# Queries and keys of the first layer projected by feature, and rotated without transposes

## The chip, the core and the metric

One core of a Trainium2 chip runs the whole program. The metric is the device time of one execution in microseconds (us). The core has five engines with a queue of instructions each: TensorE (PE) multiplies matrices and transposes, VectorE (DVE) and ScalarE (ACT) work element by element, GpSimd (POOL) does small side work, SyncE (SP) issues transfers. Each engine takes its instructions strictly in the order in which the program was built; an instruction that waits for another engine holds up all that stands behind it in its own queue.

## The reference

A decoder trunk of two layers over 256 tokens with 1024 features, all in float32. Layer 0 attends with 16 heads of 64 features and a causal mask (with 256 tokens there is one block, so the block selection picks nothing else). Layer 1 attends in a sliding window of 128 with four shared key and value heads. Each attention is followed by a gated feed-forward part with a causal convolution. Partial rotary turns the first 16 features of every head:

```python
h = rmsnorm(x, attn_norm[l])
q, k, v = jnp.split(h @ w_qkv_a[l], 3, axis=-1)
q = partial_rope(heads(q, N_HEADS), cos, sin)   # first 16 of 64 features of a head:
k = partial_rope(heads(k, N_HEADS), cos, sin)   # r1 = x1*cos - x2*sin, r2 = x2*cos + x1*sin
o = moba_attention(to_bhsd(q), to_bhsd(k), to_bhsd(heads(v, N_HEADS)))
x = x + o @ w_o
x = x + conv_ffn(rmsnorm(x, ffn_norm[l]), ...)
```

## The kernel before

**Split products.** Every float32 operand of a large product is split into a high part and a low part (what the high part leaves over), and each product is made of three matmuls: high with high, high with low, low with high. Activations lie transposed, with features on the partitions (`hT`).

**Weight units.** The weights come in units of 128 x 2048 elements. For a unit, `prepare` puts pieces of two kinds into the queues: ACT copies a piece to its high part (`hi_part`, L157) and DVE subtracts to get the low part (`lo_part`, L160). The early units are cut into four quarters of 512 columns, later ones into two halves of 1024. Four units can be held at once. Units 2 and 3 hold the queries and keys of the first group of four heads, 4 and 5 those of the second group, 6 and 7 of the third, 8 and 9 half of the values, 10 and 11 the fourth group.

**Order.** The order of the instructions is written out by a clock of planned time: `chain` puts a list of steps with delays off, `tick` advances the clock by what PE is planned to do and issues the steps that have become due, and `require` issues a chain at once where its result is needed. At the start and in the first projections PE, ACT, DVE and SP keep exactly the order in which the Python code issues; `manual.close()` in `attention` ends that, and from there a scheduler may move instructions past each other.

**Layer 0.** After half of the values, `qk_group(0, ...)` projects the first group of queries and keys, with tokens as output rows (`proj`: the activations are the stationary operand, 512 weight columns move). The result goes through `rotate`: ACT copies it from PSUM and scales it by the token's reciprocal norm (`qk_out`, L869), DVE turns 16 of each 64 features (`rope`, L346 to L352, with the tables `cs` and `sn`), PE transposes four blocks of 128 x 128 (`to_feature`, L358), ACT takes the high part and DVE the low part of the transposes (L369, L364). `spread` copies the keys' parts of the first 128 tokens into a block-diagonal tile on POOL (`kd`, L847). `attention` then runs scores (L402 to L409), softmax on DVE and ACT, transposes of the probabilities (`probs_T`, L463) and the products with the values (`values`, L486); in between, `fill` takes projections of the next groups from `filler`, by the numbers of `rate`.

**Tables.** `tables` (L817 to L823) makes cosine and sine: DVE, POOL, one ACT sine (L819) and four small POOL operations.

**Norms.** `row_bcast` spreads the reciprocal norm of the tokens over all partitions with a product of `ones` and a diagonal tile (L715), ahead of each feed-forward part.

Of the kernel before, what the change touches and what calls it, by code (L numbers as in the profile page):

```python
# [14 lines left out]
P = 128  # L15
D = 1024
S = 256
# [43 lines left out]
def trunk(ctx: ExitStack, tc, x, xw, pos, cpk, fin, sinks, w, out):  # L61
# [309 lines left out]
    def rotate(o, n, b, hi, lo, key, copy, then=None, wait=750.0):  # L371
# [3 lines left out]
              (wait, lambda: rope(t.rearrange("p (h d) -> p h d", d=HD), 2 * n, b)),  # L375
              (1000.0, lambda: to_feature(t, n, b, hi, lo, key, then)))

    def attention(qk, ready, filler, lead, rate, msk, vcol, sink):


# [116 lines left out]
        fill(lead)  # L497
        manual.close()
        n_g = NH // 4
        state = scores(0)  # L500
        for g in range(n_g):
            pT = []
            for p in range(2):
                fill(rate(g)[p])
                pT.append(probs_T(2 * g + p, state[p]))
            fill(rate(g)[2])
            if g + 1 < n_g:
                state = scores(g + 1)
            values(g, pT)
        for _ in filler:  # L510
            pass
        return oT
# [195 lines left out]
    def row_bcast(rb, b):  # L708

        r = rstd_of(b)  # L710
        d = row3(P)

        def spread():
            t = bank("t")
            nc.tensor.matmul(t[:, :P], ones, d, start=True, stop=True)  # L715
# [3 lines left out]
        chain(("rb", b), (2000.0, lambda: nc.vector.tensor_scalar(out=d, in0=ident, scalar1=r, scalar2=None, op0=ALU.mult)),  # L719
              (300.0, spread))  # L720
# [56 lines left out]
    def first_parts(c):  # L777
        hi, lo = hx(hT, c)
        (src, raw), g = chunk(c), (g1 if c > 1 else g0)[:, c:c + 1]
        wh, wl = (t[:, (c % 4) * 512:(c % 4 + 1) * 512] for t in wq[c // 4])  # L780
        if c == 0:
            nc.vector.tensor_copy(wh, raw)
        nc.scalar.activation(hi, src, AF.Copy, scale=g)
        if c > 0:
# [51 lines left out]
            v_out(b, 0, v_acc[b])  # L836

    chain(("rs",), (3000.0, first_norm))
    chain(("tables",), (3010.0, tables))
    used(0)  # L840
    used(1)

# [21 lines left out]

    qk = {}

    def qk_out(t, b, o):
        require("rs")
        nc.scalar.activation(t, o, AF.Copy, scale=rs[b])  # L869

    def qk_group(g, u):
        hi, lo = quad(), quad()
        o = [bank("acc") for _ in range(NB)]

        def finish(b):
            rotate(o[b], 4, b, hi, lo, ("qk", g), lambda t: qk_out(t, b, o[b]),
                   None if b else lambda src, w: spread(g, src[:, 2:4], w), 750.0 if g else 450.0)

        gens = [proj(o[b], hT, b, cols512(u), (u, u + 1) if b else ()) for b in range(NB)]
        if g == 0:  # L880
            for pair in zip(*gens):
                yield sum(pair)
            finish(0)
            finish(1)
        else:
            for b in range(NB):
                yield from gens[b]
                finish(b)
        qk[g] = (hi[:, 0:2], lo[:, 0:2], hi[:, 2:4], lo[:, 2:4], lambda p: p, diagonal(g))

    def run(gen):
# [77 lines left out]
    def ready_b(oT):  # L969
        o_down.append(Down(U_OB, 4, oT, lambda i: require("o", i)))  # L970

    attention(qk, ready_b, filler_b(), 3500.0, lambda g: ((4200.0, 2200.0, 1400.0), (3200.0, 1800.0, 1200.0), (3200.0, 1800.0, 1200.0), (4000.0, 1800.0, 1500.0))[g], mask, lambda h: 2 * (h // 8) + h % 2, True)

    hT = new_hT()
    y = [quad(F32, "y") for _ in range(2)]
# [144 lines left out]
```

## Time and profile before

| | |
|---|---|
| median of 3 runs | 571.14 us (571.11 to 572.1) |
| the profiled execution | 570.39 us |
| its span, first to last instruction | 568.3 us |
| busy in the span | PE 98%, DVE 75%, ACT 67%, POOL 18% |
| mean granted TensorE clock | 0.999 |

The span is shorter than the execution's time by 2.1 us of start and end. A row of the timeline gives start and duration in us, engine, source line, operation, written and read tiles, shapes and count; what stands in brackets at its end is the idle time of the engine ahead of it and what ended that. Matmuls overlap in the pipeline, so the cost of one is the distance from its start to the next one's, not its duration. A window's row gives, for each engine, busy time and (x) instructions.

### The profile page before, as it was taken

How to read it: one execution, taken by the hardware profiler on the slowest of the kernel's cores; microseconds unless marked ns; L12 is line 12 of the kernel's file. 1: busy time of each engine (PE TensorE's matmuls, PEld its weight loads, DVE VectorE, ACT ScalarE, POOL GpSimd, SP SyncE). 2: the span in 40 equal slices, each digit the busy share in tenths (PEclk: the TensorE clock that was granted, in tenths of full speed). 3: DMA queues.
4: the chain of work that ended last, by engine and by line, in shares of the span. 5: the costliest groups of instructions: out<-in, count | busy, mean ns of one | idle time of the engine just before them, and what ended most of it. 6: DMA issues, size and time to landing. Idle time of an engine off the chain costs nothing.

```text
span 568.3 us, 10191 instructions
## 1 busy us (share of the span) xinstructions
PE 558.8 (98%) x3858; PEld 504.5 (89%) x3858; DVE 427.1 (75%) x927; ACT 380.0 (67%) x768; POOL 100.3 (18%) x124
## 2 busy tenths in 40 slices
PE   8999999999999999999999999999999999999995
PEld 7888888899999999988888988879999999988884
DVE  6798678599788888744469988788898888773414
ACT  6988777578577776743449798877667777663313
POOL 7321001011333321100002200001333332110003
PEclk9999999999999999999999999999999999999999
DMA  8974344442565565664542714242466655565201
GB/s 326 374 277 154 144 148 149 149 149 76 213 216 202 206 211 213 217 203 177 219 148 96 276 76 149 74 149 76 149 223 223 221 206 198 230 221 205 92 0 74
DMA packets 15311, 100.99 MB, mean 178 GB/s; under 512 B 1952, under 2 KB 2080, under 8 KB 3744
## 3 DMA queue, kind: packets, MB, share of 16 engines
q1 hardware_dynamic: 14976, 100.09, 48.4%
q8 instruction: 30, 0.49, 0.3%
q10 hardware_dynamic: 288, 0.26, 0.1%
q14 instruction: 17, 0.14, 0.1%
HBM read 99.30 MB, written 1.05 MB: 177 GB/s over the span
## 4 chain that ended last, share of the span: by engine, by line
PE 88%; DVE 5%; ACT 4%; issue 1%; POOL 1%; DMA 1%; DVEq 0%; POOLq 0%; ACTq 0%
PE acc L533 9%; PE acc L538 9%; PE acc L534 9%; PE u L628 6%; PE u L629 6%; PE u L627 6%; PE t L628 6%; PE t L629 6%; PE t L627 6%; PE acc L317 4%; PE acc L319 4%; PE acc L318 4%; PE acc L739 2%; PE acc L628 2%; PE acc L629 2%; PE acc L627 2%
## 5 line engine op out<-in xcount | busy, mean ns | idle before, releaser
L160 DVE TENSOR_TENSOR wl<-wr,wh 128x1024 fp32r<-128x1024 f32 (+1 forms) x208 | 221.0, 1080 | 68.1 <-ACT wh L157 67.7
L157 ACT ACTIVATE wh<-wr 128x1024 fp32r<-128x1024 f32 (+1 forms) x208 | 190.0, 946 | 75.0 <-PE acc L538 55.4
L533 PE MATMUL acc<-wh,q 128*128 128x512 f32 x238 | 94.5, 397 | 0.8 <-ACT q L492 0.7
L534 PE MATMUL acc<-wl,q 128*128 128x512 f32 x238 | 92.9, 390 | 0.0
L671 POOL TENSOR_TENSOR m<-m,m 128x256 f32<-128x256 f32 x44 | 60.2, 1367 | 182.2 <-DVE m L666 109.2
L628 PE MATMUL u<-q,wh 128*128 128x256 f32 x320 | 88.5, 277 | 0.0
L627 PE MATMUL u<-q,wh 128*128 128x256 f32 x320 | 88.2, 276 | 0.0
L629 PE MATMUL u<-q,wl 128*128 128x256 f32 x320 | 88.1, 275 | 0.0
L629 PE MATMUL t<-q,wl 128*128 128x256 f32 x288 | 79.2, 275 | 0.0
L627 PE MATMUL t<-q,wh 128*128 128x256 f32 x288 | 79.2, 275 | 0.0
L628 PE MATMUL t<-q,wh 128*128 128x256 f32 x288 | 79.2, 275 | 0.0
L538 PE MATMUL acc<-wh,q 128*128 128x512 f32 x238 | 76.9, 389 | 0.0
L628 PEld LDWEIGHTS u<-q,wh 128*128 128x128 f32 x320 | 60.1, 188 | 0.1
L627 PEld LDWEIGHTS u<-q,wh 128*128 128x128 f32 x320 | 60.0, 188 | 0.1
L629 PEld LDWEIGHTS u<-q,wl 128*128 128x128 f32 x320 | 60.1, 188 | 0.0
L317 PE MATMUL acc<-wh,q 128*128 128x512 f32 (+1 forms) x160 | 57.1, 357 | 0.0
L319 PE MATMUL acc<-wh,q 128*128 128x512 f32 (+1 forms) x160 | 55.4, 346 | 0.0
L318 PE MATMUL acc<-wl,q 128*128 128x512 f32 (+1 forms) x160 | 55.2, 345 | 0.0
L627 PEld LDWEIGHTS t<-q,wh 128*128 128x128 f32 x288 | 54.1, 188 | 0.0
L628 PEld LDWEIGHTS t<-q,wh 128*128 128x128 f32 x288 | 54.1, 188 | 0.0
L629 PEld LDWEIGHTS t<-q,wl 128*128 128x128 f32 x288 | 54.1, 188 | 0.0
L533 PEld LDWEIGHTS acc<-wh,q 128*128 128x128 f32 x238 | 44.7, 188 | 10.5 <-ACT q L492 1.6
(165 smaller groups left out, 995.1 us busy)
## 6 DMA issues: line engine op xcount, KB each, us to landing
wr<-in_w SPq DMA_DIRECT2D x90, 1024.0 KB, 4.8
first<-in_xw SPq DMA_DIRECT2D x5, 384.0 KB, 5.6
xr<-in_x SPq DMA_DIRECT2D x2, 512.0 KB, 8.3
first<-in_xw SPq DMA_DIRECT2D x1, 768.0 KB, 7.0
fin_t<-in_fin SPq DMA_DIRECT2D x1, 512.0 KB, 6.2
out<-ot SPq DMA_DIRECT2D x1, 512.0 KB, 2.6
first<-in_xw SPq DMA_DIRECT2D x1, 388.0 KB, 3.6
out<-m ACTq DMA_DIRECT2D x1, 256.0 KB, 2.1
```

Source lines behind the costliest of these rows:

```text
L157: nc.scalar.activation(wq[i][0][:, c], raws[i][:, c], AF.Copy)
L160: nc.vector.tensor_tensor(out=wq[i][1][:, c], in0=raws[i][:, c], in1=f(wq[i][0][:, c]), op=ALU.subtract)
L317: nc.tensor.matmul(o, xh[:, blk(b)], wh, start=(c == 0), stop=False)
L318: nc.tensor.matmul(o, xh[:, blk(b)], wl, start=False, stop=False)
L319: nc.tensor.matmul(o, xl[:, blk(b)], wh, start=False, stop=(c == KC - 1))
L533: nc.tensor.matmul(o, ph[:, blk(b)], hi[:, s_], start=first, stop=False)
L534: nc.tensor.matmul(o, ph[:, blk(b)], lo[:, s_], start=False, stop=False)
L538: nc.tensor.matmul(o, pl[:, blk(b)], hi[:, s_], start=False, stop=end)
L627: nc.tensor.matmul(o, hi[:, s_], xh, start=(c == 0), stop=False)
L628: nc.tensor.matmul(o, hi[:, s_], xl, start=False, stop=False)
L629: nc.tensor.matmul(o, lo[:, s_], xh, start=False, stop=(c == KC - 1))
L671: nc.gpsimd.tensor_tensor(out=h, in0=gs, in1=t[1], op=ALU.mult)
```

## The change

There are five parts.

1. In layer 0, `proj_f` takes the place of `proj` for queries and keys. Now 128 weight columns are the stationary operand and all 256 tokens move, so the result already lies by feature. A group has a bank for the keys (first) and one for the queries, of two times 256 columns each. `rotate_f` then turns on whole banks: a DVE shuffle of partitions swaps the halves of the rotated features (L419), three DVE operations multiply with the tables and add (L420 to L422), ACT takes the high part (L425), DVE the low part (L430). The ACT copy with the norm, the rope on 16 features and the transposes are gone.
2. The norm is now inside the tables. `new_tables` builds on POOL a tile with cosine and sine for every feature of two heads (ones and zeros where nothing turns: L383 to L387), ACT scales it by the norm (L393), PE transposes it in four blocks (L399), ACT copies it to SBUF (L404).
3. In both attentions, PE's order of scores, probabilities' transposes and values is fixed as written, with the second pair of transposes, the filler, the next scores and the values as one fixed stretch. The last group's `rate` in layer 1 goes from 4000, 1800, 1500 to 3600, 1200, 600.
4. In layer 0 both copies of the transposed probabilities are on ACT.
5. `row_bcast` issues its product 1500 instead of 300 planned ns behind the diagonal tile, and the second chunk of the first value weights is split between ACT and DVE.

```diff
+    def new_tables(rs_, key, *wait):
+        ex = mid().rearrange("p (b k e d) -> p b k e d", b=NB, k=2, e=2)
+        nc.gpsimd.memset(ex[:, :, 0, :, ROT:], 1.0)
+        nc.gpsimd.memset(ex[:, :, 1, :, ROT:], 0.0)
+        for k, t in enumerate((cs, sn)):
+            for e in range(2):
+                nc.gpsimd.tensor_copy(ex[:, :, k, e, :ROT], t)
...
+        def scale():
+            for b in range(NB):
+                nc.scalar.activation(sc[:, b], ex[:, b].rearrange("p k e d -> p k (e d)"), AF.Copy, scale=rs_[b])
+        def turn():
+            t = bank("t")
+            for b in range(NB):
+                for k in range(2):
+                    nc.tensor.transpose(t[:, k * S + b * P:k * S + (b + 1) * P], sc[:, b, k], ident)
+            tick(440)
+            chain(key, (300.0, lambda: copy(t)))
+        def copy(t):
+            nc.scalar.activation(new, t.rearrange("p (k t) -> p k t", k=2), AF.Copy)
+            tab[0] = new
+        chain(key, *wait, (0.0, scale), (1200.0, turn))
+    def rotate_f(o, hi, lo, key, tkey, then=None):
...
+        def turn():
+            require(*tkey)
+            c_, s_ = (tab[0][:, k].unsqueeze(1).to_broadcast([P, 2, S]) for k in range(2))
+            nc.vector.stream_shuffle(u, o, SWAP)
+            nc.vector.tensor_tensor(out=t3, in0=o3, in1=c_, op=ALU.mult)
+            nc.vector.tensor_tensor(out=u3, in0=u3, in1=s_, op=ALU.mult)
+            nc.vector.tensor_tensor(out=t, in0=t, in1=u, op=ALU.add)
+        def high():
+            nc.scalar.activation(hi, t3, AF.Copy)
...
+        def low():
+            nc.vector.tensor_tensor(out=lo, in0=t3, in1=f(hi), op=ALU.subtract)
...
+        chain(key, (150.0, turn), (2600.0, high), (700.0, low))
+    def proj_f(o, hT, wv, units=()):
+        for m in range(2):
+            om = o[:, m * S:(m + 1) * S]
+            for c in range(KC):
...
+                nc.tensor.matmul(om, wh, xh, start=(c == 0), stop=False)
+                nc.tensor.matmul(om, wh, xl, start=False, stop=False)
+                nc.tensor.matmul(om, wl, xh, start=False, stop=(c == KC - 1))
...
-                    if e:
+                    if e or not sink:
                         nc.scalar.activation(pT, tp[:, :3 * P], AF.Copy)
...
+            with tc.manual_schedule(engines={mybir.EngineType.PE}):
+                pT.append(probs_T(2 * g + 1, state[1]))
+                fill(rate(g)[2])
+                if g + 1 < n_g:
+                    state = scores(g + 1)
+                values(g, pT)
...
-              (300.0, spread))
+              (1500.0, spread))
...
+    def tables_a():
+        tables()
+        new_tables(rs, ("rt",))
+    chain(("rt",), (3010.0, tables_a))
...
+        gens = [proj_f(o[n], hT, cols128(u, 2, S - n * S), (u, u + 1) if n else ()) for n in range(2)]
         if g == 0:
+            for _ in range(KC):
+                yield sum(next(gen) for gen in gens)
+        for n in range(2):
+            yield from gens[n]
+            finish(n)
```

**Place 1: PE in the first group's projection.** Before, PE goes straight from the first group (banks acc_282 and acc_283) to the second (acc_381):

```order
L317 MATMUL acc_283<-wh_252,q_107 128x512
L318 MATMUL acc_283<-wl_253,q_107 128x512
L319 MATMUL acc_283<-wh_252,q_108 128x512
L317 MATMUL acc_381<-wh_329,q_105 128x512
L318 MATMUL acc_381<-wl_330,q_105 128x512
```

Now the table's transposes (L399, reading the scaled tile m_23_349) stand inside the first group, ahead of the last chunk of the first column half; 42 matmuls of this group stand ahead of them; behind them come three of the keys' bank acc_283, three of the queries' bank acc_284, then 24 and 24:

```order
L445 MATMUL acc_284<-q_107,wh_253 128x256
L446 MATMUL acc_284<-q_108,wh_253 128x256
L447 MATMUL acc_284<-q_107,wl_254 128x256
L399 MATMUL t_369<-ident,m_23_349 128x128 x4
L445 MATMUL acc_283<-q_107,wh_253 128x256
L446 MATMUL acc_283<-q_108,wh_253 128x256
L447 MATMUL acc_283<-q_107,wl_254 128x256
```

What PE had no part in before, the tables, now has four instructions in the middle of its queue.

**Place 2: ACT around the sine.** Before, the second group's first weight unit (wh_329) follows the sine (L819) at once:

```order
L743 ACTIVATE v_101<-acc_113,rstd_304 128x512
L743 ACTIVATE v_102<-acc_114,rstd_313 128x512
L819 ACTIVATE rb<-rb 128x32
L157 ACTIVATE wh_329<-wr_237 128x512 x4
L157 ACTIVATE wh_362<-wr_250 128x512 x2
```

Now the scaling of the table stands between them, and the copy of the transposed table (L404) behind the unit's second quarter (wh_359 is the same unit 4, wh_415 unit 5):

```order
L831 ACTIVATE v_102<-acc_114,rstd_329 128x512
L910 ACTIVATE rb<-rb 128x32
L393 ACTIVATE m_23_349<-m_22_342,rstd_320 128x256
L393 ACTIVATE m_23_349<-m_22_342,rstd_329 128x256
L157 ACTIVATE wh_359<-wr_238 128x512 x2
L404 ACTIVATE tab_350<-t_369 128x512
L157 ACTIVATE wh_359<-wr_238 128x512 x2
L157 ACTIVATE wh_415<-wr_251 128x512 x3
L425 ACTIVATE q_281<-m_26_410 128x512
```

ACT now takes the second group's first weights only behind the two scalings (L393), which read what POOL's four copies (L387) write.

**Place 3: DVE at the second group's weights.** Before, the rotation of the first group is eight small operations between the quarters of units 4 (wl_330) and 5 (wl_363):

```order
L160 TENSOR_TENSOR wl_330<-wr_237,wh_329 128x512 x4
L160 TENSOR_TENSOR wl_363<-wr_250,wh_362 128x512 x2
L346 TENSOR_TENSOR rb<-m_22_377,cs 128x128
L351 TENSOR_TENSOR rb<-m_22_377,sn 128x8x8 x2
L352 TENSOR_TENSOR m_22_377<-rb 128x8x16
```

Now the last quarter of unit 4 (wl_360) stands behind the rotation of the keys' bank, and the last two quarters of unit 5 (wl_416) behind that of the queries' bank:

```order
L160 TENSOR_TENSOR wl_360<-wr_238,wh_359 128x512 x3
L419 STREAM_SHUFFLE m_27_411<-acc_283 128x512
L420 TENSOR_TENSOR m_26_410<-acc_283,tab_350 128x512
L421 TENSOR_TENSOR m_27_411<-m_27_411,tab_350 128x512
L422 TENSOR_TENSOR m_26_410<-m_26_410,m_27_411 128x512
L160 TENSOR_TENSOR wl_360<-wr_238,wh_359 128x512
L160 TENSOR_TENSOR wl_416<-wr_251,wh_415 128x512 x2
L419 STREAM_SHUFFLE m_29_450<-acc_284 128x512
L420 TENSOR_TENSOR m_28_449<-acc_284,tab_350 128x512
L421 TENSOR_TENSOR m_29_450<-m_29_450,tab_350 128x512
L422 TENSOR_TENSOR m_28_449<-m_28_449,m_29_450 128x512
L160 TENSOR_TENSOR wl_416<-wr_251,wh_415 128x512 x2
```

Weight pieces that the second group needs have moved behind operations that wait for the first group's banks.

More of the change, by code (lines that the diff above doesn't have):

```diff
@@ L376, in rotate @@
               (1000.0, lambda: to_feature(t, n, b, hi, lo, key, then)))
+    tab = [None]
+    def new_tables(rs_, key, *wait):
[5 more added lines that the diff above has]
+                nc.gpsimd.tensor_copy(ex[:, :, k, e, :ROT], t)
+        sc = mid().rearrange("p (b k f) -> p b k f", b=NB, k=2)
+        new = quad(F32, "tab")[:, :2]
+        def scale():
[12 more added lines that the diff above has]
+        chain(key, *wait, (0.0, scale), (1200.0, turn))
@@ new lines, in trunk @@
+    SWAP = [(i + HALF) % ROT if i < ROT else i for i in range(32)]
+    def rotate_f(o, hi, lo, key, tkey, then=None):
+        t, u = mid(), mid()
+        t3, u3, o3 = (a.rearrange("p (c t) -> p c t", c=2) for a in (t, u, o))
+        def turn():
[7 more added lines that the diff above has]
+            nc.scalar.activation(hi, t3, AF.Copy)
+            if then is not None:
+                then(hi, 0)
+        def low():
+            nc.vector.tensor_tensor(out=lo, in0=t3, in1=f(hi), op=ALU.subtract)
+            if then is not None:
+                then(lo, 1)
+        chain(key, (150.0, turn), (2600.0, high), (700.0, low))
@@ new lines, in proj_f @@
+    def proj_f(o, hT, wv, units=()):
+        for m in range(2):
+            om = o[:, m * S:(m + 1) * S]
+            for c in range(KC):
+                for b in range(NB):
+                    require("x", b, c // 4)
+                xh, xl = hx(hT, c)
+                wh, wl = wv(c, m)
+                nc.tensor.matmul(om, wh, xh, start=(c == 0), stop=False)
+                nc.tensor.matmul(om, wh, xl, start=False, stop=False)
+                nc.tensor.matmul(om, wl, xh, start=False, stop=(c == KC - 1))
+                tick(3 * S / 2.4)
+                if m and units and (c + 1) * len(units) % KC == 0:
+                    used(units[(c + 1) * len(units) // KC - 1])
+                yield 3 * S / 2.4
@@ L378, in attention, with cols128, wv @@
+    def cols128(u, n_u, at):
+        def wv(c, m):
+            i, r = divmod(c * n_u, KC)
+            need(u + i)
+            w_ = UNIT * n_u // KC
+            s_ = slice(r // n_u * w_ + at + m * P, r // n_u * w_ + at + (m + 1) * P)
+            return tuple(t[:, s_] for t in wq[u + i])
+        return wv
     def attention(qk, ready, filler, lead, rate, msk, vcol, sink):
@@ L499, in attention @@
         n_g = NH // 4
-        state = scores(0)
+        with tc.manual_schedule(engines={mybir.EngineType.PE}):
+            state = scores(0)
         for g in range(n_g):
             pT = []
[L503 to L509, printed above, removed]
+            fill(rate(g)[0])
+            pT.append(probs_T(2 * g, state[0]))
+            fill(rate(g)[1])
+            with tc.manual_schedule(engines={mybir.EngineType.PE}):
+                pT.append(probs_T(2 * g + 1, state[1]))
[3 more added lines that the diff above has]
+                values(g, pT)
         for _ in filler:
@@ L783, in first_parts @@
         nc.scalar.activation(hi, src, AF.Copy, scale=g)
-        if c > 0:
+        if c == 1:
+            nc.scalar.activation(wh[:, :S], raw[:, :S], AF.Copy)
+            nc.vector.tensor_copy(wh[:, S:], raw[:, S:])
+        elif c > 1:
             nc.scalar.activation(wh, raw, AF.Copy)
@@ L838, in trunk @@
     chain(("rs",), (3000.0, first_norm))
-    chain(("tables",), (3010.0, tables))
+    def tables_a():
+        tables()
+        new_tables(rs, ("rt",))
+    chain(("rt",), (3010.0, tables_a))
     used(0)
@@ L865, in trunk, with finish @@
     qk = {}
-    def qk_out(t, b, o):
-        require("rs")
-        nc.scalar.activation(t, o, AF.Copy, scale=rs[b])
     def qk_group(g, u):
         hi, lo = quad(), quad()
[L873 to L879, printed above, removed]
-        if g == 0:
[L881 to L888, printed above, removed]
+        o = [bank("acc") for _ in range(2)]
+        def finish(n):
+            c = slice(2 - 2 * n, 4 - 2 * n)
+            rotate_f(o[n], hi[:, c], lo[:, c], ("qk", g), ("rt",), None if n else lambda src, w: spread(g, src, w))
+        gens = [proj_f(o[n], hT, cols128(u, 2, S - n * S), (u, u + 1) if n else ()) for n in range(2)]
+        if g == 0:
+            for _ in range(KC):
[3 more added lines that the diff above has]
+            finish(n)
         qk[g] = (hi[:, 0:2], lo[:, 0:2], hi[:, 2:4], lo[:, 2:4], lambda p: p, diagonal(g))
@@ L970, in ready_b @@
         o_down.append(Down(U_OB, 4, oT, lambda i: require("o", i)))
-    attention(qk, ready_b, filler_b(), 3500.0, lambda g: ((4200.0, 2200.0, 1400.0), (3200.0, 1800.0, 1200.0), (3200.0, 1800.0, 1200.0), (4000.0, 1800.0, 1500.0))[g], mask, lambda h: 2 * (h // 8) + h % 2, True)
+    attention(qk, ready_b, filler_b(), 3500.0, lambda g: ((4200.0, 2200.0, 1400.0), (3200.0, 1800.0, 1200.0), (3200.0, 1800.0, 1200.0), (3600.0, 1200.0, 600.0))[g], mask, lambda h: 2 * (h // 8) + h % 2, True)
     hT = new_hT()
```

## The prediction

> **What bounds the kernel now.** I read the page's busy times and its chain first, then windows, then PE's timeline.
>
> ```profile
> span 568.3 us, 10191 instructions
> PE 558.8 (98%) x3858; PEld 504.5 (89%) x3858; DVE 427.1 (75%) x927; ACT 380.0 (67%) x768; POOL 100.3 (18%) x124
> PE 88%; DVE 5%; ACT 4%; issue 1%; POOL 1%; DMA 1%; DVEq 0%; POOLq 0%; ACTq 0%
> ...
> 14.00:28.00 14.00, 14.00 (x64) 11.58 (x63) 10.41 (x23) 12.66 (x27) 4.51 (x11) 1.00 0.93 372
> 28.00:42.00 14.00, 14.00 (x79) 11.74 (x78) 13.19 (x37) 12.22 (x21) 4.05 (x8) 1.00 0.76 285
> 440.00:500.00 60.00, 60.00 (x532) 60.00 (x531) 50.39 (x83) 43.02 (x71) 14.73 (x12) 1.00 0.60 217
> ```
>
> The reader is to see two things. PE is never short of work for long, so work taken from it shortens the end, and a wait put into its queue lengthens it: there is no idle time later to absorb one. And from 28 to 42 us, where the first heads are rotated, DVE (the third busy time) is at 13.19 of 14 us. Work added there has no room.
>
> **PE's work.** The timeline gives what a projection and a group of transposes cost.
>
> ```profile
> 16.41 0.39 PE L317 MATMUL acc<-wh,q 128*128 128x512 f32 x1
> ...
> 26.84 0.39 PE L318 MATMUL acc<-wl,q 128*128 128x512 f32 x1
> 30.01 1.03 PE L358 MATMUL t<-ident,m 128*128 128x128 f32 x8
> ...
> 44.75 0.60 PE L358 MATMUL t<-ident,m 128*128 128x128 f32 x4
> 45.10 0.47 PE L317 MATMUL acc<-wh,q 128*128 128x512 f32 x1
> 45.42 0.39 PE L318 MATMUL acc<-wl,q 128*128 128x512 f32 x1
> ```
>
> A matmul with 512 moving columns costs (26.84 - 16.41) / 46 = 227 ns. One with 256, in the feed-forward part, costs 60 / 532 = 113 ns (window 440 to 500). Queries and keys have 192 of the first, and now 384 of the second: 43.5 against 43.3 us, so -0.2. Four transposes cost 45.42 - 44.75 - 0.23 = 0.44 us with the matmul that they delay. Eight such groups go and one (the tables) comes: -7 x 0.44 = **-3.1**.
>
> **The wait for the tables.** This is the first of two terms that decide. The rows of ACT and POOL around the sine:
>
> ```profile
> 22.33 0.69 ACT L743 ACTIVATE v<-acc,rstd 128x512 f32<-128x512 f32 x1 [0.47 <-POOL rstd L303]
> 22.92 0.22 ACT L819 ACTIVATE rb<-rb 128x32 f32<-128x32 f32 x1
> 23.04 2.18 ACT L157 ACTIVATE wh<-wr 128x512 fp32r<-128x512 f32 x4
> 45.25 0.89 ACT L448 ACTIVATE m<-m,hst 128x256 f32<-128x256 f32 x2
> ...
> 23.20 0.20 POOL L822 COPY cs<-rb 128x16 f32<-128x16 f32 x1 [0.61 <-ACT rb L819]
> 23.73 0.77 POOL L823 TENSOR_SCALAR sn<-rb 128x16 f32<-128x16 f32 x1
> 4.41 0.45 POOL L758 COPY g<-first 128x8 f32<-128x8 f32 x1 [0.99 <-DMA first<-in_xw]
> ```
>
> Nothing that leads to the sine is changed: it starts at 22.9 us, and sine and cosine lie ready at 24.5. Then come four POOL copies (0.2 to 0.45 us each by L822 and L758, so 24.7 to 26.3 with some overlap; I take 25.2), two ACT scalings of 256 columns (0.45 each by L448: 26.1), and the last transposes with a handover: PE can go on at 26.4. Without the wait it would come to the transposes at 16.41 + 42 x 0.113 = 21.15 and be through at 21.6. So PE stands still for **+4.8** (4.3 to 5.9 from the ends above). Before, the first PE instruction that needed the tables (L358) came at 30.0 us. Whatever the split second chunk saves at the head only makes this wait longer, so I cost it at nothing.
>
> **The wait for DVE.** DVE's prices:
>
> ```profile
> 14.81 4.99 DVE L160 TENSOR_TENSOR wl<-wr,wh 128x512 fp32r<-128x512 f32 x8 [0.30 <-ACT wh L157]
> 28.58 0.29 DVE L346 TENSOR_TENSOR rb<-m,cs 128x128 f32<-128x128 f32 x1
> 28.79 0.35 DVE L351 TENSOR_TENSOR rb<-m,sn 128x64 f32<-128x64 f32 x2
> 29.18 0.29 DVE L352 TENSOR_TENSOR m<-rb 128x128 f32<-128x128 f32 x1
> 29.39 1.28 DVE L160 TENSOR_TENSOR wl<-wr,wh 128x512 fp32r<-128x512 f32 x2
> 31.28 0.69 DVE L364 TENSOR_TENSOR q<-t,q 128x512 fp32r<-128x512 f32 x1 [0.60 <-ACT q L369]
> 31.89 1.35 DVE L160 TENSOR_TENSOR wl<-wr,wh 128x1024 fp32r<-128x1024 f32 x1
> ...
> L782 DVE CAST wh<-first 128x512 fp32r<-128x512 f32 x1 | 0.4, 427 | 3.3 <-DMA first<-in_xw 3.3
> ...
> 133.72 0.84 POOL L671 TENSOR_TENSOR m<-m,m 128x256 f32<-128x256 f32 x1 [10.45 <-ACT m L670]
> 133.87 1.23 DVE L643 TENSOR_TENSOR q<-y,q 128x512 fp32r<-128x512 f32 x1
> ```
>
> An operation on two times 512 columns takes 4.99 / 8 = 0.62 from SBUF and 31.89 - 31.28 = 0.61 with PSUM. The old rotation cost 29.39 - 28.58 + 0.61 = 1.4 us of DVE for each block of 512. The new one has five operations, 3.1 us if the shuffle, which no row shows, costs like the others. Its bounds: 0.35 by the plain copy L782 less the usual overlap, 1.23 by L643, which ran beside POOL. It reads PSUM like L364, so I take 0.62. Four of the five are one turn of 2.5 us.
>
> Let PE go on behind the tables' transposes at R. The keys' bank needs 30 more matmuls, R + 3.4, and 0.2 to DVE. The turn of the keys ends at R + 6.1, the last quarter of unit 4 at R + 6.7, two quarters of unit 5 at R + 8.0, the turn of the queries at R + 10.5, the third quarter at R + 11.1, the fourth at R + 11.7. PE ends the first group at R + 54 x 0.113 = R + 6.1 and uses one quarter every 0.34 us; the low part of the seventh chunk (unit 5, third quarter) is wanted at R + 6.1 + 6 x 0.34 + 0.23 = R + 8.35. It waits 2.75, and 0.25 more at the next chunk: **+3.0** (2.4 to 4.3 by the shuffle's bounds, counted twice). Nothing of this depends on R. If the tables' transposes stood later on PE, DVE would still begin the keys' turn only after the third quarter (about 29 us, since ACT holds unit 4 back behind the tables), and PE would wait some 6.5 us at that chunk instead of 4.8 + 3.0.
>
> Behind that, DVE arrives at the softmax of groups 0 and 1 about when PE wants the probabilities. One copy of probabilities per pair moves from DVE to ACT and helps it there; ACT has room for the eight moved copies, since it loses as many copies of 512 columns (L869). I add **+0.7** (0 to 2) for waits of this kind. SP issues the transfer of a unit behind the last low part of an earlier one, so transfers slip with DVE; three raw units lie in stock, and I cost that at nothing.
>
> **Savings elsewhere.** The stalls that the other edits touch:
>
> ```profile
> 123.74 0.46 PE L715 MATMUL t<-m,ones 128*128 128x128 f32 x2 [0.28 <-DVE m L719]
> 387.61 0.46 PE L715 MATMUL t<-m,ones 128*128 128x128 f32 x2 [0.27 <-DVE m L719]
> ...
> 336.51 0.44 PE L358 MATMUL t<-ident,m 128*128 128x128 f32 x2 [0.42 <-DVE m L352]
> 373.33 0.50 PE L533 MATMUL acc<-wh,q 128*128 128x512 f32 x1 [0.69 <-ACT q L492]
> ```
>
> The later `row_bcast` puts eight or nine more matmuls (1.0 us) ahead of each L715, which covers both waits: **-0.6** (0 if the later `rb` makes DVE's scaling late). In layer 1 the values of the last group come six matmuls of 512 (1.4 us) earlier, so ACT's copy has cover, but its probabilities are also wanted 1.4 us earlier; the transposes at 336 us move away from the scores. Of 0.42 + 0.69 I take **-0.6** (-1.1 to +0.7).
>
> **The sum:** -0.2 - 3.1 + 4.8 + 3.0 + 0.7 - 0.6 - 0.6 = +4.0. The profiled execution took 570.39, so 574.4 in its terms; the median of the runs, 571.14, lies 0.75 above it, so **575.1** for the median. The ends: -3.3 + 4.3 + 2.4 + 0 - 0.6 - 1.1 = +1.7 (572.8) and -3.3 + 5.9 + 4.3 + 2 + 0 + 0.7 = +9.6 (580.7), not all at once.
>
> **Rivals.**
>
> The clock falls during PE's wait.
>
> ```profile
> 1.11 3.48 PE L251 MATMUL u<-ones 128*128 128x128 f32 x16 [1.11 <-DVE warm L227]
> 123.74 0.46 PE L715 MATMUL t<-m,ones 128*128 128x128 f32 x2 [0.28 <-DVE m L719]
> 123.95 0.36 PE L629 MATMUL u<-q,wl 128*128 128x256 f32 x1
> ...
> 561.83 0.28 PE L595 MATMUL u<-wh,q 128*128 128x256 f32 x1
> ...
> 562.20:567.20 5.00, 0.00 (x0) 0.00 (x0) 1.97 (x6) 1.31 (x4) 0.55 (x1) 1.00 0.48 184
> 567.50:568.30 0.80, 0.00 (x0) 0.00 (x0) 0.00 (x0) 0.00 (x0) 0.00 (x0) 0.50 0.00 0
> ```
>
> The same pair of records takes 0.21 us at 123.74 and 0.43 at the start, for 3.5 us: the array starts at half speed. At the end the granted clock was still 1.00 five us after the last matmul, and lower after that. PE's wait is idle for about 4.4 us. If the clock fell, some 3.5 us at half speed would cost +1.7, and DVE's turn would come later by as much: 576.8. The trace speaks rather against it; 15%. [...]
>
> DVE stays short through groups 0 and 1. If its new operations take over 0.75 us on average (L643's 1.23 beside POOL, whose `kd` copies fall into the turns), the softmax of group 1 comes after PE's transposes want it. Ten operations (two blocks' rotations) at 0.3 more each are +3.0, 578.1; 12%.
>
> The waits are shorter: POOL's copies overlap, the shuffle is as cheap as L782, the savings come in full: about 571.9, no change; 10%.
>
> The change does what it says and neither wait comes: -3.3 - 1.2 gives 566.6, faster. It needs the tables on ACT before 21 us, while the sine starts at 22.9, and a DVE with 2 x 2.5 us free where it has 0.8; 6%.
>
> My forecast holds the other 57%. The range reaches from the short waits to the long DVE queue: 571.5 to 579.0. A measurement of this kernel tells 0.2% (1.1 us) from no change, so 570.0 to 572.3 is no change: faster 0.06, same 0.12, slower 0.82.
>
> **What would show it.** Right: a PE gap of 4 to 6 us ahead of L399, released by ACT L393, at 21 us; a second gap of 2 to 4 us at a matmul L447 near 34 us, released by DVE L160; DVE over 13 of 14 us from 28 to 56; L358 down from 52 to 20 records. Wrong: PE idle under 2 us before 45 us, or shuffles (L419) well under 0.5 us with the quarters of unit 5 early. If both gaps are there and the time is still under 571, a saving elsewhere was missed.

## The result

The changed kernel takes 577.78 us (median of four runs, 576.3 to 578.27), the kernel before 571.12 us beside it: a ratio of 1.0108, with a 95% interval from 1.0087 to 1.013. That is 6.7 us slower, inside the predicted range and 2.7 us above the predicted time. The profiled execution took 577.91 us.

The page of the changed kernel, its busy times and the granted clock in 40 slices:

```profile
span 576.2 us, 10530 instructions
PE 560.7 (97%) x4022; PEld 514.7 (89%) x4022; DVE 438.0 (76%) x928; ACT 379.5 (66%) x771; POOL 103.5 (18%) x130
PEclk9889999999999999999999999999999999999998
```

The second and third digits of the last row are 8: the clock, which was 1.00 there before, fell early in the program. Two answers of windows over the changed kernel, the first with the stretches that the prediction used, the second cut where the granted clock changes (after the window: PE, PEld, DVE, ACT and POOL busy with their instructions, then the clock):

```profile
14.00:28.00 14.00, 10.25 (x68) 9.47 (x67) 7.67 (x17) 11.44 (x26) 4.27 (x17) 0.85 0.91 367
28.00:42.00 14.00, 11.37 (x79) 10.79 (x79) 10.49 (x19) 6.80 (x11) 2.52 (x3) 0.87 0.26 83
...
23.73:30.55 6.82, 5.21 (x25) 5.10 (x26) 1.99 (x3) 5.03 (x10) 1.19 (x8) 0.50 0.42 171
...
40.79:44.21 3.42, 3.42 (x18) 3.42 (x17) 3.38 (x4) 1.80 (x2) 2.07 (x2) 0.50 0.80 278
44.21:70.00 25.79, 25.79 (x225) 24.39 (x225) 24.73 (x63) 19.23 (x40) 4.99 (x8) 1.00 0.47 168
```

PE was busy for 14.00 of 14 us in the first two windows before, and now for 10.25 and 11.37. Twice the clock is at half, for 6.82 and 3.42 us, and from 44 to 70 us PE is busy without a break, although DVE is at 24.73 of 25.79. The whole loss arises before 44 us. PE's timeline shows its two waits and what a matmul costs behind the first:

```profile
21.32 0.28 PE L447 MATMUL acc<-q,wl 128*128 128x256 f32 x1
25.34 1.12 PE L399 MATMUL t<-ident,m 128*128 128x128 f32 x4 [3.75 <-ACT m L393]
...
26.47 0.41 PE L446 MATMUL acc<-q,wh 128*128 128x256 f32 x1
26.68 0.41 PE L447 MATMUL acc<-q,wl 128*128 128x256 f32 x1
...
36.22 0.28 PE L446 MATMUL acc<-q,wh 128*128 128x256 f32 x1
36.59 0.39 PE L447 MATMUL acc<-q,wl 128*128 128x256 f32 x1
...
36.93 0.28 PE L446 MATMUL acc<-q,wh 128*128 128x256 f32 x1
39.74 0.39 PE L447 MATMUL acc<-q,wl 128*128 128x256 f32 x1 [2.54 <-DVE wl L160]
```

By starts, the wait for the tables is 25.34 - 21.32 - 0.11 = 3.9 us. The wait for DVE is 39.74 - 36.93 - 0.11 = 2.7 us, with 36.59 - 36.22 - 0.11 = 0.26 ahead of it and 0.14 at the next chunk: 3.1 us. Behind the first, a matmul starts 26.68 - 26.47 = 0.21 us after the one before it instead of 0.113; so it is again from 40.8 to 44.2 us. The first fall comes at 23.73 us, still within the wait; of the 6.82 us at half clock PE works for 5.21. What released the first, on ACT and POOL:

```profile
23.09 0.22 ACT L910 ACTIVATE rb<-rb 128x32 f32<-128x32 f32 x1
24.78 0.91 ACT L393 ACTIVATE m<-m,rstd 128x256 f32<-128x256 f32 x2 [1.48 <-POOL m L387]
```

```profile
23.90 0.25 POOL L914 TENSOR_SCALAR sn<-rb 128x16 f32<-128x16 f32 x1
24.39 0.36 POOL L387 COPY m<-sn 128x32 f32<-128x32 f32 x2
```

And DVE's rows ahead of the quarter for which PE waits the second time:

```profile
31.89 0.74 DVE L419 STREAM_SHUFFLE m<-acc 128x512 f32<-128x512 f32 x1
32.52 0.68 DVE L420 TENSOR_TENSOR m<-acc,tab 128x512 f32<-128x512 f32 x1
33.11 0.69 DVE L421 TENSOR_TENSOR m<-m,tab 128x512 f32<-128x512 f32 x1
33.84 0.69 DVE L422 TENSOR_TENSOR m<-m,m 128x512 f32<-128x512 f32 x1
34.44 2.09 DVE L160 TENSOR_TENSOR wl<-wr,wh 128x512 fp32r<-128x512 f32 x3
36.47 0.73 DVE L419 STREAM_SHUFFLE m<-acc 128x512 f32<-128x512 f32 x1
...
39.00 1.29 DVE L160 TENSOR_TENSOR wl<-wr,wh 128x512 fp32r<-128x512 f32 x2
```

The order is the one forecast: the keys' turn, the last quarter of unit 4 with two of unit 5, the queries' turn, then the third quarter at 39.00, behind which PE goes on at 39.74. A turn takes 34.44 - 31.89 = 2.55 us, and the shuffle costs 0.63 of it, like its neighbours.

### The profile page after: what moved, and what is told of

It is laid out like the page before. It is cut to its first block, busy times and chain, and to the rows that moved or that the text cites. A ratio compares the mean times of both kernels' runs of the same rounds, so it can differ in the third digit from the quotient of the medians.

```text
span 576.2 us, 10530 instructions
## 1 busy us (share of the span) xinstructions
PE 560.7 (97%) x4022; PEld 514.7 (89%) x4022; DVE 438.0 (76%) x928; ACT 379.5 (66%) x771; POOL 103.5 (18%) x130
## 3 DMA queue, kind: packets, MB, share of 16 engines
HBM read 99.30 MB, written 1.05 MB: 174 GB/s over the span
## 4 chain that ended last, share of the span: by engine, by line
PE 89%; ACT 3%; DVE 3%; DMA 2%; issue 1%; POOL 1%; SPq 0%; DVEq 0%; POOLq 0%; ACTq 0%
PE acc L621 9%; PE acc L622 9%; PE acc L626 9%; PE u L715 6%; PE u L717 6%; PE u L716 6%; PE t L717 6%; PE t L715 6%; PE t L716 6%; PE acc L447 2%; PE acc L445 2%; PE acc L446 2%; PE acc L715 2%; PE acc L717 2%; PE acc L716 2%; PE acc L317 2%
## 5 line engine op out<-in xcount | busy, mean ns | idle before, releaser
L759 POOL TENSOR_TENSOR m<-m,m 128x256 f32<-128x256 f32 x44 | 63.8, 1449 | 177.2 <-DVE m L754 111.6
L621 PEld LDWEIGHTS acc<-wh,q 128*128 128x128 f32 x238 | 44.7, 188 | 9.6 <-issue 0.9
L626 PEld LDWEIGHTS acc<-wh,q 128*128 128x128 f32 x238 | 44.7, 188 | 9.3
L622 PEld LDWEIGHTS acc<-wl,q 128*128 128x128 f32 x238 | 44.7, 188 | 8.5 <-issue 0.2
L763 ACT ACTIVATE q<-m 128x256 fp32r<-128x256 f32 x44 | 18.1, 415 | 38.7 <-POOL m L759 38.7
```

The costliest lines, as they stand in the source:

```text
L621: nc.tensor.matmul(o, ph[:, blk(b)], hi[:, s_], start=first, stop=False)
L622: nc.tensor.matmul(o, ph[:, blk(b)], lo[:, s_], start=False, stop=False)
L626: nc.tensor.matmul(o, pl[:, blk(b)], hi[:, s_], start=False, stop=end)
L759: nc.gpsimd.tensor_tensor(out=h, in0=gs, in1=t[1], op=ALU.mult)
L763: (3400.0, lambda: nc.scalar.activation(hi, h, AF.Copy)),
```

## The experiments

All edits are to the changed kernel unless another is named. The kernel before, run beside them on the same chips, took 570.7 to 570.9 us. The first four take the two waits and the clock apart.

**Work for PE in the first wait.**

```diff
         def turn():
+            warm_up(20)
             t = bank("t")
```

> The changed kernel with 20 small matmuls of a constant tile put on PE right ahead of the tables' transposes, so that the array works through some 2 us of the wait; their result is not used. Theory (the clock falls because PE idles, and a slow stretch from 26.1 to 30.55 us costs 2.1 to 2.4 us): the wait for the tables keeps its length, since the sine and the scaling are where they were, the granted clock stays at 1.00 until 36 us, the wait at the seventh chunk of the second group stays at about 3.0 us, and the time falls from 577.8 to about 575.3. Rival, the record of the clock has nothing to do with PE's idling: half clock at 24 us again and 577.8. Rival, what PE gains before the first turn is given back at the seventh chunk: full clock at 24 us, a wait of about 5 us at the chunk, 577.8.

574.84 us (573.9 to 575.49). The timeline of PE in this run:

```profile
20.95 4.62 PE L251 MATMUL u<-ones 128*128 128x128 f32 x40
25.41 0.66 PE L400 MATMUL t<-ident,m 128*128 128x128 f32 x4
...
37.40 0.39 PE L448 MATMUL acc<-q,wl 128*128 128x256 f32 x1 [2.53 <-DVE wl L160]
```

The small matmuls fill the whole wait (20 of them leave 40 records and 4.46 us, not the 2 us I had taken), the transposes start no earlier, and the wait for DVE is 2.7 us as before. The clock stayed at 1.00 behind the tables (from 26 to 31 us, where the changed kernel has 0.54), and the time fell by 2.9 us. So in this kernel the slow clock came from PE's standing still. The four runs differ in the other fall, as far as the mean granted clock tells: two of them have 0.997 (573.9 and 574.46 us) and two 0.994 (575.22 and 575.49). The latter two, with the first fall alone gone, lie 2.4 us under the changed kernel, which is the expected price. In the profiled one, with 0.997, the clock did not fall behind the wait for DVE either (1.00 from 36 to 46 us), with the same wait of 2.7 us.

**Work in both waits.** The second place, `warm_at`, is the seventh chunk of the keys of the second group.

```diff
                 nc.tensor.matmul(om, wh, xl, start=False, stop=False)
+                if (m, c) == warm_at:
+                    warm_up(20)
                 nc.tensor.matmul(om, wl, xh, start=False, stop=(c == KC - 1))
```

> The same small matmuls a second time, ahead of the low part of the seventh chunk of the second group, where PE waits for DVE. Theory: both waits as they were (3.9 and about 3.0 us), no half clock anywhere, and another 1.6 us less than with the first lot alone: about 573.7, which is 2.6 above the kernel before and is the two waits less the saved transposes. If the 20 matmuls are not enough to count as work, the second fall stays and the time is that of the run with the first lot.

575.67 us: a miss of 2.0 us, by my price. The second lot takes 39.45 - 35.07 = 4.4 us by PE's starts, where the wait holds 2.7, and so makes PE late by 1.7 us itself. By the mean clock (0.997 to 0.999 in all runs, where the changed kernel has 0.989 to 0.991) neither fall came. With lots cut to the waits, 17 and 11:

> The run with two lots of small matmuls, with the lots cut to what the waits hold: 20 took 4.46 us of full clock, so 17 (3.8 us) ahead of the tables' transposes and 11 (2.45 us) ahead of the seventh chunk. Theory (each wait keeps its length and only the slow stretches go): no half clock before the end in any run, scores of the first group at about 44.0 us as in the run with the first lot, and every run near the lowest of that one: 573.9 to 574.3. The changed kernel then carries 577.8 - 574.0 = 3.8 us of slow clock and 3 us of bare waits over the saved transposes. Rival, the slow clock costs less and the runs with the first lot alone were only scattered: a median of 574.8 again, with a spread of 1.5.

574.21 us, and all four runs between 573.94 and 574.52 with a clock of 0.997 or above. The timeline:

```profile
21.07 3.96 PE L251 MATMUL u<-ones 128*128 128x128 f32 x34
25.19 0.84 PE L400 MATMUL t<-ident,m 128*128 128x128 f32 x4 [0.17 <-ACT m L393]
34.65 2.62 PE L251 MATMUL u<-ones 128*128 128x128 f32 x22
37.34 0.38 PE L450 MATMUL acc<-q,wl 128*128 128x256 f32 x1
```

Both waits are about as long as in the changed kernel (25.19 - 21.07 = 4.1 and 37.34 - 34.65 = 2.7 us), only filled. What is left out against it is the slow clock alone: 577.78 - 574.21 = **3.6 us**. Held against the kernel before that ran beside each of them (571.12 and 570.69) it is 3.1. The traces say 3.7, by the stage from the first projection to the first scores, which takes 27.65 us with filled waits (the row stands with the old turns below) and 31.33 us in the changed kernel:

```profile
16.66:47.99 31.33, 24.95 (x176) 24.07 (x175) 20.94 (x39) 16.73 (x33) 6.83 (x18) 0.84 0.51 197
```

**Tables ready early.** The scaling and the transposes of the tables run ahead of the first group, on constants.

```diff
+    new_tables((1.0, 1.0), ("rt",))
     v_first(KC - 1)
...
-    chain(("rt",), (3010.0, tables_a))
+    chain(("tables",), (3010.0, tables))
```

> The tables hold ones and zeros without sine, cosine or norm, so the rotation and the scaling with the norm are left out of the result; every instruction of the turns stays. The tables' scaling and transposes run before the first group, so PE has nothing to wait for there; POOL's four small copies are gone. Theory (the wait for DVE does not depend on the wait for the tables): no gap ahead of the first group's last chunk, no half clock at 24 us, but the wait of about 3 us at the seventh chunk of the second group and the fall of the clock behind it stay; 577.8 - 3.9 - 0.3 - 2.3 = about 571.3. Rival, DVE is late only because the tables are late: the second wait goes as well, about 566.7.

573.72 us. It is 2.4 above the forecast of the theory, mostly since the moved transposes still waited for ACT's scaling, 19.48 - 17.53 - 0.11 = 1.84 us by starts, and a quarter ahead of the seventh chunk another 0.3. The two sides that were to be told apart are told apart, by PE's timeline and a window:

```profile
19.48 0.74 PE L396 MATMUL t<-ident,m 128*128 128x128 f32 x4 [1.68 <-ACT m L390]
35.39 0.39 PE L444 MATMUL acc<-q,wl 128*128 128x256 f32 x1 [2.53 <-DVE wl L160]
```

```profile
36.70:40.12 3.42, 3.42 (x19) 3.42 (x18) 3.11 (x3) 1.54 (x2) 1.98 (x2) 0.50 0.88 307
```

With the tables out of the way the wait for DVE is still 2.7 us, and the clock still falls behind it. DVE is not late because the tables are late.

**A light turn.** The shuffle, the second product and the sum are left out, and with them the rotation.

```diff
-            nc.vector.stream_shuffle(u, o, SWAP)
             nc.vector.tensor_tensor(out=t3, in0=o3, in1=c_, op=ALU.mult)
-            nc.vector.tensor_tensor(out=u3, in0=u3, in1=s_, op=ALU.mult)
-            nc.vector.tensor_tensor(out=t, in0=t, in1=u, op=ALU.add)
```

> The turn has one DVE operation instead of four (the product with the first table); shuffle, product with the second table and sum are left out, and with them the rotation itself. The tables are made and waited for as in the changed kernel. Theory: the wait for the tables and the half clock behind it stay, the wait at the seventh chunk (3.0 us) goes, since 2 x 1.9 us of DVE work ahead of that quarter are gone, and with it the second fall of the clock (1.6): about 573.2. Rival, the second fall is an after-effect of the first: half clock again at about 38 to 41 us, 574.8. Rival, the quarter waits for ACT and not for DVE: about 577.

572.14 us (ten runs, 571.6 to 574.54). PE's and DVE's timelines, and a window:

```profile
20.73 0.28 PE L444 MATMUL acc<-q,wl 128*128 128x256 f32 x1
25.02 1.12 PE L399 MATMUL t<-ident,m 128*128 128x128 f32 x4 [4.01 <-ACT m L393]
```

```profile
30.69 0.69 DVE L419 TENSOR_TENSOR m<-acc,tab 128x512 f32<-128x512 f32 x1 [2.56 <-PE acc L444]
...
33.41 0.69 DVE L419 TENSOR_TENSOR m<-acc,tab 128x512 f32<-128x512 f32 x1
```

```profile
24.93:28.34 3.41, 3.33 (x16) 3.21 (x17) 1.99 (x3) 3.41 (x8) 0.00 (x0) 0.50 0.63 256
```

The wait for the tables is there, and one slow stretch behind it; the wait for DVE and the second slow stretch are gone (from 28.43 to 37.18 us a matmul starts every 0.11 to 0.12 us, and the mean clock is 0.995 where the changed kernel has 0.989). So DVE's turns make the second wait, and the second fall is no after-effect of the first. In this profile the clock was at half for 3.41 us only, against 6.82 in the changed kernel, which fits a time 1.1 us under the forecast. It is the profile of the shortest of the ten runs; two of the others have a mean granted clock of 0.990, as low as in the changed kernel (572.72 and 573.17 us), and what happened there is not shown.

**Tables asked for later.**

```diff
-        chain(key, *wait, (0.0, scale), (1200.0, turn))
+        chain(key, *wait, (0.0, scale), (5200.0, turn))
```

> The changed kernel with the tables' transposes asked for 5200 instead of 1200 planned ns behind the scaling: on PE they now stand behind all of the keys' bank of the first group (75 matmuls ahead of them instead of 42), at about 25.2 us, when the scaled tables are ready. Theory (the wait is DVE's in the end, and the tables' wait only takes a part of it in advance): nearly no wait at the transposes and full clock until 30 us, but DVE begins the keys' turn only at about 28 us, so the seventh chunk of the second group is waited for until about 35.5 us, 5 to 6 us instead of 3, with one or two slow stretches behind it; 573.5 to 574.5. Rival, the wait for the tables and its slow clock are the whole excess and the wait at the seventh chunk stays at 3.0: 577.8 - 3.9 - 0.3 - 2.3 = about 571.3.

574.28 us (573.61 to 574.99). PE's timeline:

```profile
25.29 0.84 PE L399 MATMUL t<-ident,m 128*128 128x128 f32 x4 [0.35 <-ACT m L393]
31.31 0.38 PE L447 MATMUL acc<-q,wl 128*128 128x256 f32 x1 [1.51 <-DVE wl L160]
...
35.86 0.58 PE L447 MATMUL acc<-q,wl 128*128 128x256 f32 x1 [2.53 <-DVE wl L160]
```

The wait for the tables is gone (0.35), and PE now waits for DVE three times, 1.7, 0.3 and 2.7 us by the starts, ahead of three quarters. The clock was at half for 6.8 us (0.50 from 34.89 to 41.72), part of it in the last of these waits. The rival's 571.3 did not come: of the 3.9 - 0.5 = 3.4 us that PE saves at the tables by starts, DVE takes back 1.6 (4.7 us of waits where the changed kernel has 3.1).

The next runs measure the rest of the change, and look for a better version.

**The old turns with everything else of the change.**

```diff
-        gens = [proj_f(o[n], hT, cols128(u, 2, S - n * S), (u, u + 1) if n else ()) for n in range(2)]
+        gens = [proj(o[b], hT, b, cols512(u), (u, u + 1) if b else ()) for b in range(NB)]
...
-    chain(("rt",), (3010.0, tables_a))
+    chain(("tables",), (3010.0, tables))
```

> The changed kernel with projection, rotation and tables of the kernel before (parts 1 and 2 undone); the fixed order in both attentions, the copies of the probabilities on ACT, the later norm product and the split second chunk stay. Theory (all of the loss is in parts 1 and 2; of the rest only the later norm product shows, 0.45 a layer): no half clock before the end, 0.9 less than the kernel before, so about 569.9 where that takes 570.8. Rival, the fixed order in layer 1 costs what the norm product saves: 570.8. Rival, part of the loss is in the other parts: over 572.

**568.85 us**, a ratio of 0.9962 (0.9949 to 0.9975) to the kernel before: faster than both kernels, and by 1.1 us better than I expected. PE has no wait over 0.2 us in layer 0, and the clock is full there. All of the loss is in parts 1 and 2. Layer 0 up to its feed-forward part, by stage, here and in the run with filled waits; each answer's first window goes from the first projection to the first scores, its second from there to the feed-forward part:

```profile
16.48:37.46 20.98, 20.98 (x100) 17.47 (x99) 16.88 (x37) 18.11 (x33) 5.64 (x12) 1.00 0.82 307
37.46:116.28 78.82, 78.82 (x468) 64.67 (x467) 55.60 (x166) 62.93 (x153) 6.57 (x13) 1.00 0.44 160
```

```profile
16.30:43.95 27.65, 27.31 (x232) 26.36 (x231) 20.57 (x38) 16.72 (x33) 6.82 (x18) 1.00 0.60 229
43.95:121.30 77.35, 77.35 (x556) 67.36 (x554) 64.77 (x173) 61.24 (x148) 8.83 (x13) 1.00 0.46 168
```

At full clock the new turns cost 6.7 us up to the first scores and win 1.5 us behind them.

**The later norm product alone**, in the kernel before.

```diff
-              (300.0, spread))
+              (1500.0, spread))
```

> The kernel before with one number changed: the product that spreads the norm is issued 1500 instead of 300 planned ns behind its diagonal tile. Theory (the gain of the run with the old turns, 2.0 us, is mostly this): both waits of 0.44 us at that product go and the feed-forward parts behind them start without the small gaps at their head, 0.5 in layer 0 and 0.9 in layer 1 by the run with the old turns: 569.4 where the kernel before takes 570.9. Rival, the gain comes from the fixed order in the attentions and the copies on ACT: 570.4.

569.6 us, a ratio of 0.998 (0.9971 to 0.999): 1.1 us of the 2.0. By starts the two waits were 123.74 - 123.18 - 0.11 = 0.45 us and 387.61 - 387.06 - 0.11 = 0.44 us; the 0.28 and 0.27 in the brackets count only from the end of the matmul before. The product that waited 0.27 us on DVE at 387.61 now stands in the timeline without a wait:

```profile
387.89 0.38 PE L715 MATMUL t<-m,ones 128*128 128x128 f32 x2
```

The other 0.7 to 0.9 us is not settled, and the intervals of the two ratios touch (0.9975 and 0.9971). The stage from the first scores to the feed-forward part is 0.2 us shorter with the fixed order and the copies on ACT than in the kernel before (78.82 against 79.04); one profile of the norm-only run also shows a wait of 0.5 us at 30.5 us, in code that is the kernel before's to the letter, so single profiles do not decide half a microsecond here.

**The fixed order undone in layer 1**, with the old turns; `sink` marks layer 1, and the last group's amounts of filler are 4000, 1800, 1500 again.

```diff
+        def fixed():
+            return ExitStack() if sink else tc.manual_schedule(engines={mybir.EngineType.PE})
...
-        with tc.manual_schedule(engines={mybir.EngineType.PE}):
+        with fixed():
             state = scores(0)
```

> The run with the old turns, with the fixed order undone in layer 1's attention alone (the scheduler orders PE there, and the last group's amounts of filler are those of before). Theory (the fixed order gains nothing in layer 1: it takes away waits of 0.58, 0.40 and 0.86 us and brings 1.38, 0.30 and 0.36): the waits of before come back and the new ones go, 568.5 to 568.9. Rival, the fixed order in layer 1 does gain, 0.6 as predicted: 569.5.

569.07 us, ratio 0.997 (0.9957 to 0.9983): no difference from the old turns with the fixed order (0.9962) that can be told. The waits of before (0.58, 0.40 and 0.86 us) are back in place of 1.38, 0.30 and 0.36. In the changed kernel the largest of the new ones is this:

```profile
341.61 0.55 PE L548 MATMUL u<-ident,m 128*128 128x128 f32 x3 [1.15 <-ACT m L554]
```

**New turns for the later groups only.** One or two groups of heads are turned in the old way, the tables are built later, and the other groups are turned in the new way.

```diff
     def qk_group(g, u):
+        if g < 2:
+            yield from qk_old(g, u)
+            return
...
-    chain(("rt",), (3010.0, tables_a))
+    chain(("tables",), (3010.0, tables))
+    chain(("rt0",), (16000.0, lambda: new_tables(rs, ("rt",))))
```

> The changed kernel with the old projection and rotation for the first two groups of heads and the new one for groups three and four; the tables are built later, where nothing waits for them. Theory: neither wait and no half clock, four groups of four transposes fewer and one more (-1.3), 0.9 for the norm products: about 568.6, 2.2 less than the kernel before. Rival, DVE is also short from 56 to 70 us (13.99 of 14 busy in the changed kernel), so the turns of the third group make PE wait there: 570 to 571.

> The same with the old way for the first group alone, so that three groups of heads are turned in the new way. Theory: the second group's turns come at about 40 us, when the early quarters of the weights are done, and make nobody wait; six groups of transposes fewer and one more (-2.2), 0.9 for the norm products: about 567.7. Rival, DVE (13.19 of 14 us busy from 28 to 42 before) has no room for one more turn there: a wait of 1 to 3 us ahead of the second group's scores, 569 to 571.

> Two groups turned in the old way and two in the new one, again with layer 1 left to the scheduler. Theory: as the run with two old groups, less at most 0.3: 568.4 to 568.9, since the transposes saved there (PE's end 0.95 us earlier than with all old turns) should show at last. Rival, what is saved in layer 0 is lost again at the end of the program: 569.0.

With two old groups: 568.95 us, ratio 0.9964 (0.9952 to 0.9976), and with layer 1 left to the scheduler as well 569.08 us. With one old group: 569.45 us, with a wait of 1.25 us ahead of the second group's scores as the rival has it, at a transposition of the first group's probabilities (L548) that is released by DVE. So two late groups in the new way cause no wait, but they do not beat the old turns in time, although PE's last matmul starts 0.95 us earlier than there (559.55 against 560.50). The end of the program took that back: the spans of the two profiled executions are 566.8 and 566.9 us. The last transfer, of 256 KB, landed 2.8 us after its issue with two old groups and 2.2 us with all old turns; in the run with two old groups and layer 1 left to the scheduler it was 2.5. Why is open; the code there is the same.

## Why the prediction was right, and where not

The direction, both waits, their places in PE's queue and their releasers came as forecast; the second began at 37 us instead of 34, behind the first slow stretch. Term by term, with the run that measures it:

| term | forecast, us | measured, us | from |
|---|---|---|---|
| wait for the tables | +4.8 | +3.9 | timeline of the changed kernel |
| wait for DVE | +3.0 | +3.1 | the same; 2.7 with early tables, gone with light turns |
| transposes and projection | -3.3 | about -2.0 | 27.65 + 77.35 (filled waits) - 20.98 - 78.82 (old turns) = 5.2, less waits of 4.1 + 3.1 there |
| softmax lateness | +0.7 | 0 | PE busy for 25.79 of 25.79 us from 44 us on, and no stall over 0.2 us before layer 1 |
| later norm product | -0.6 | -1.1 | norm alone |
| layer 1's attention | -0.6 | 0 | fixed order undone in layer 1 |
| slow clock | a rival, +1.7 | +3.6 | filled waits |
| rest of the change | 0 | -0.7 to -0.9 | old turns, less the norm; cause open |

The measured column adds up to +3.9 + 3.1 - 2.0 - 1.1 + 3.6 - 0.8 = +6.7. Several of its terms are differences between the same runs, so that it closes is no check of its own.

**The step that failed** is the first rival: "If the clock fell, some 3.5 us at half speed would cost +1.7", at 15%, with the remark that the trace speaks rather against it. The clock fell during the wait for the tables, for 6.8 us where the rival's estimate has 3.5, and it fell a second time, for 3.4 us, behind the wait for DVE, which I had not thought of as a candidate at all, since it is shorter. Two errors lie in it. I read from the end of the old trace that five idle microseconds leave the clock at 1.00, and took the wait as safe; and I left it out of the sum as another course of events, where it is a cost on top of the two waits. Without the slow clock the changed kernel takes 574.2 us, 0.9 under the predicted 575.1. That this lies so near is in part luck: the terms that came out lower than forecast (the wait for the tables, the softmax, the norm product, the rest of the change) do so by 2.9 us in all, and the others (the wait for DVE, the transposes, layer 1) came out 2.0 us higher.

**Sizes that were off.** The wait for the tables was put 0.9 too high: the fourth POOL operation ran for 0.25 us, not 0.77, so the copies began at 24.09 us instead of 24.5, and PE came to the transposes a little later, at 21.43 us instead of 21.15. The four copies took 0.7 us together, as assumed. The transposes were put 1.3 too high. Behind the first scores five groups go, by my price 2.2 us, and the stage became 1.5 us shorter. In layer 1 the moved values did lose their waits, but the second pair of transposes now waits 1.3 us for ACT's copy: an exchange, as the run without it shows. The later norm product was put at the idle times in the brackets, 0.28 and 0.27, where its two waits are 0.45 and 0.44 us by starts; the 0.2 that is left to 1.1 is within the noise.

One sign that I had named did not show: DVE over 13 of 14 us from 28 us on. It was busy for 10.49 of the first 14 and 12.91 of the next, since at half clock PE was late with the keys' bank, and DVE stood waiting for it (3.44 us ahead of 31.89).

**Steps that held to the tenth.** The shuffle's price (0.62 taken, 0.63 measured), the turn of 2.5 us, the place and the length of the wait for DVE, and that nothing of it depends on R: 2.7 us in the changed kernel, with early tables and with PE kept busy. That later transposes of the tables would only move the wait to DVE was said as "some 6.5 us at that chunk"; it came as 4.7 us over three quarters. DVE, nearly full from 44 to 70 us (24.73 of 25.79), made nobody wait there: that rival did not come.

## What to carry to other kernels

When a wait is put into the queue of an engine that was always busy, price the time after it as well: where the clock fell, the matmuls behind waits of 2.7 to 4.2 us ran at half clock for 3.3 to 5.9 us, and that was about half of this loss (3.1 to 3.7 of 6.7). A wait that is taken away is not gained in full where the engine that is late next has no room: with the tables asked for later, PE waited 4.7 us for DVE instead of 3.1. Look at what that engine has queued ahead of the wanted piece. And where an edit has several parts, run the side parts alone: here they were worth 2.0 us, and were hidden under a loss of 8.9.

## What was not expected of the hardware

The four changes of the clock in the first 70 us of the changed kernel, at 23.73, 30.55, 40.79 and 44.21 us, lie 6.82, 10.24 and 3.42 us apart: 2, 3 and 1 times 3.41. So I counted PE's work in windows of that length, laid out from a change that the trace shows: in the changed kernel, in the run with early tables (a change at 36.70 us), in the run with late tables (34.89), and in the kernel before at its end (567.34):

```profile
20.31:23.73 3.42, 1.29 (x12) 1.09 (x10) 0.66 (x5) 2.52 (x7) 2.10 (x7) 1.00 1.02 386
23.73:27.14 3.41, 1.80 (x9) 1.69 (x10) 0.90 (x2) 2.36 (x6) 1.19 (x8) 0.50 0.81 333
37.38:40.79 3.41, 1.05 (x6) 0.86 (x7) 3.38 (x6) 1.67 (x3) 0.00 (x0) 1.00 0.55 228
```

```profile
16.23:19.64 3.41, 1.73 (x14) 1.50 (x13) 3.41 (x7) 3.10 (x7) 0.00 (x0) 1.00 1.03 424
```

```profile
31.48:34.89 3.41, 1.67 (x9) 1.07 (x9) 3.38 (x7) 1.30 (x2) 1.38 (x2) 1.00 0.75 257
34.89:38.30 3.41, 2.44 (x11) 2.44 (x12) 3.41 (x6) 3.06 (x4) 1.22 (x1) 0.50 0.34 82
```

```profile
560.51:563.93 3.42, 1.59 (x13) 1.35 (x12) 2.19 (x7) 1.93 (x6) 1.64 (x2) 1.00 0.38 153
563.93:567.34 3.41, 0.00 (x0) 0.00 (x0) 1.01 (x2) 0.51 (x1) 0.00 (x0) 1.00 0.42 154
```

The run with work in the first wait shows the same wait of 2.7 us without a fall. With the clock at 1.00 on both sides no change shows where its windows begin; with the bounds below, which are a choice of mine, two of them share the wait, from 34.70 to 37.40 us:

```profile
32.71:36.13 3.42, 2.07 (x16) 1.67 (x15) 3.39 (x8) 1.62 (x3) 1.47 (x2) 1.00 0.66 218
36.13:39.54 3.41, 2.14 (x16) 1.95 (x17) 3.41 (x5) 2.76 (x4) 0.93 (x1) 1.00 0.43 130
```

The clock fell behind windows in which PE was busy for 1.29, 1.05 and 1.67 us (and 1.31 ahead of the fall with early tables), and not behind windows with 1.73 and 1.59 us, nor behind those with 2.07 and 2.14, whose bounds no change fixes. It was still at half behind windows with 1.80 and 2.44 us of work, and back at full behind windows with 3.33 (light turn), 3.41 and 3.42 us. A wait of 2.7 us was enough for a fall where the window that held it had 1.05 us of work, or 1.31 with early tables. The busy times are modelled and the cases few; the 1.67 ahead of a fall and the 1.59 ahead of none show that the busy time alone does not tell the cases apart. The two rows of the kernel before also show what I misread: the five us of full clock behind the old kernel's last matmul were the rest of a window with 1.59 us of work and one with 0.00, at whose end, at 567.34 us, the clock fell to 0.50.

The fall does not come at the same place of the wait in all profiles, nor at the same cost. In the changed kernel it came 23.73 - 21.32 - 0.11 = 2.3 us into the wait for the tables, with the light turn 24.93 - 20.73 - 0.11 = 4.1 us. There a whole window held 0.00 us of work (21.51 to 24.93), PE came back at the head of the next, and the clock was back after 3.41 us instead of 6.82. With the first wait filled, two runs have a mean clock of 0.997 and two 0.994, and the latter take 1.2 us more; that this is the fall behind the second wait is my estimate, since no trace shows one of the slower two. The record of the clock has a gap of its own: in the kernel before it says 1.00 for the first 4 us too, where a pair of records took 0.43 us and later 0.21. In the slow stretches behind the two waits the pace of the matmuls (0.21 us instead of 0.113) confirms it.
